# First stage of a two-block network: subtractions and scan sums moved from GpSimd to VectorE

## The chip, the cores and the metric

The kernel runs on one core of one Trainium2 chip. The metric is the device time of one launch in microseconds (us). In this text TensorE is PE, VectorE is DVE, ScalarE is ACT, GpSimd is POOL and SyncE is SP, as the profile has them. Each engine works through its own queue of instructions strictly in order and waits at an instruction until what that one needs is there.

## The reference, cut to what matters

Two blocks of different design follow each other on 512 tokens of width 1024. The change lies in the first block, in its state-space branch and in the multiplication of weights.

```python
def s5_ssm(u, a_re, a_im, log_dt, b_re, b_im, c_re, c_im, d, glu_w, glu_b):
    ...
    bu_r = jnp.einsum('blgp,gnp->blgn', uf, bbar_r)
    bu_i = jnp.einsum('blgp,gnp->blgn', uf, bbar_i)
    ...
    _, _, s_r, s_i = lax.associative_scan(_complex_linear_combine, (a_r, a_i, bu_r, bu_i), axis=1)
    y = (jnp.einsum('blgn,gpn->blgp', s_r, c_re.astype(jnp.float32))
         - jnp.einsum('blgn,gpn->blgp', s_i, c_im.astype(jnp.float32))
         + d.astype(jnp.float32).reshape(SSM_GROUPS, SSM_CH) * uf)
    z = jax.nn.gelu(y.reshape(B, L, SSM_WIDTH), approximate=False)
    z = z * jax.nn.sigmoid(z @ glu_w.astype(jnp.float32) + glu_b.astype(jnp.float32))
    return z.astype(u.dtype)

def first_block(...):
    ...
        proj = rms_norm(h, norm1_g[l]) @ w_in[l]
        attn = sliding_window_attention(...)
        ssm = s5_ssm(...)
        mixed = jnp.concatenate([rms_norm(attn, attn_out_g[l]), rms_norm(ssm, ssm_out_g[l])], axis=-1)
        h = h + mixed @ w_out[l]
        h = h + peer_ffn(...)
```

The scan is a complex linear recurrence over 528 positions (16 meta tokens and 512 tokens), with 32 groups of 64 states. After the first block come a feed-forward layer with 16,384 single-neuron experts (peer_ffn) and the second block of two layers, which also reads a memory of 256 rows through keys and values made from weights.

## The kernel before, in words

**Weights in two parts.** Every large matrix product is made of three passes: the weight is loaded as 128x1024 float32 (tile `wraw`), rounded on ACT to a high part (`whi`, line 267), and the rest is a subtraction (`wlo`, line 268). `mm3` multiplies high by high, low by high and high by low (lines 273 to 275). The class `Stream` does this in a fixed order of weights: three `wraw` buffers are loaded ahead, and three `whi` and `wlo` buffers are split ahead. Its field `lo_eng` says which engine subtracts: POOL where it is set, DVE where it is None.

**The first stage** (`phase_a`) runs two Python generators against each other. `ssm()` has 16 turns T, two groups of the scan each; `fill_a()` yields pieces of all other work: `proj_qkv`, then `attention` (four blocks i of 128 tokens), then `memory` (32 weight columns, 24 products with tile `pk` each, 768 in all), then `mix_out` (tile `po`). `finish_a` comes after both: the gate of the state-space branch (tile `pg`), its half of the output product, and the norm. What the queues finally hold is set by a scheduler that lays all instructions on a simulated time line and orders each engine's queue by it, so an edit in one place can move instructions far from it.

**One turn of the scan.** `table(T)` makes the cosine and sine of 528 positions from two short tables: four products on POOL (lines 653 to 656), one subtraction and one sum on DVE (657, 658). `bu(T)` multiplies on PE (671) and takes each PSUM result times the tables on DVE (673 to 677), combines (679, 680), scans twice (`tensor_tensor_scan`, 683 and 684), multiplies the states by the tables again (687 to 690), and then adds and subtracts these products on POOL:

```python
            g.tensor_tensor(n[0], n[0], n[1], op=OP.add)
            g.tensor_tensor(n[2], n[2], n[3], op=OP.subtract)
```

`y(T)` multiplies both sums on PE (703, 704), and every fourth turn DVE adds the skip term into `uT` (707), which `finish_a` puts through Gelu. One attention block reads scores of PE on DVE (817), takes the softmax through ACT (827, 836) and DVE (831, 832), transposes and multiplies on PE (849, 851, 855), and splits the result (`ahl`, 862 and 863), which `mix_out` needs.

**Before the turns** `norm_in` and `proj_u` normalise the input and project it; their first weights are subtracted on POOL. `ssm_params` makes the angles in eight 128x736 operations on POOL (tile `eq`, 557 to 564), from which ACT takes sine and cosine (569 to 571). `memory_in` puts two small norm chains (319 to 324) into the same queue. In `memory` every call of the stream sets `lo_eng` to POOL, so its 32 weight columns are subtracted there.

**After the stage** `phase_p1` computes expert scores; its DVE routes tokens and handles 128 gathered rows (`ring`, line 1116) and then 128 sums (`sacc`, 1126) for the first token tile. `phase_p2` multiplies the second expert matrix (tile `acc`), and its first step on DVE is line 1289.

Of the kernel before, what the change touches and what calls it, by code (L numbers as in the profile page):

```python
# [17 lines left out]
OP = mybir.AluOpType  # L18
# [185 lines left out]
class Stream:  # L204
# [38 lines left out]
    def next(self, held=0):  # L243

        n = self.n_used
        self._split(n + 1 + self.ahead - held)
        self.n_used += 1
        return self.got.pop(n)


class Kernel:
# [249 lines left out]
    def proj_u(self):  # L501
        nc = self.nc
        self.uT = self.pa.tile([128, 4, L], F32, name="uT")
        norm = self.norm_in()
        for cs in ((0, 1), (2,), (3,)):
            self.W.lo_eng = nc.gpsimd if cs[0] < 1 else None
            ws = [self.W.next(held=j) for j in range(len(cs))]
            for o in HALVES:
                next(norm, None)
                for c, w in zip(cs, ws):  # L510
                    ps = self.proj(w, *o)
                    nc.scalar.copy(self.uT[:, c, o[0]:o[1]], ps)
# [126 lines left out]
    def ssm(self):  # L639
        nc, pa = self.nc, self.pa  # L640
        v, g, pe = nc.vector, nc.gpsimd, nc.tensor
        NA, NB = self.NA, self.NB
        new = lambda n, b=2, w=L: pa.tile([128, w], F32, name=n, tag="s_" + n, bufs=b)
        live = {}

        def table(T):

            sh = [128, NA, NB]
            cA, sA = (x[:, T, :NA, None].to_broadcast(sh) for x in (self.cosS, self.nsinS))
            cB, sB = (x[:, T, None, NA:].to_broadcast(sh) for x in (self.cosS, self.nsinS))  # L650
            c, s, t1, t2 = new("c"), new("s"), new("t1", 1), new("t2", 1)
            r = lambda x: x.rearrange("p (a b) -> p a b", a=NA)
            g.tensor_tensor(r(c), cA, cB, op=OP.mult)
            g.tensor_tensor(r(t1), sA, sB, op=OP.mult)
            g.tensor_tensor(r(s), sA, cB, op=OP.mult)
            g.tensor_tensor(r(t2), cA, sB, op=OP.mult)
            v.tensor_tensor(c, c, t1, op=OP.subtract)
            v.tensor_tensor(s, s, t2, op=OP.add)
            live[T] = [c, s]

        def bu(T):
            a, b = divmod(T, 4)
            c, s = live[T]
            bT = pa.tile([128, 2, 128], F32, name="bT", bufs=2)
            nc.sync.dma_start(out=bT, in_=self.a["bT"][T])
            m = [new(f"m{i}", 1) for i in range(4)]
            for h in range(2):
                hs = slice(h * 264, h * 264 + 264)
                for i in range(2):
                    p = self.ps.tile([128, 264], F32, tag="bu", name="bu", bufs=2)  # L670
                    pe.matmul(p, bT[:, i], self.uT[:, a, hs], start=True, stop=True)
                    if i == 0:
                        v.tensor_tensor(m[0][:, hs], p, c[:, hs], op=OP.mult)
                        v.tensor_tensor(m[3][:, hs], p, s[:, hs], op=OP.mult)
                    else:
                        v.tensor_tensor(m[1][:, hs], p, s[:, hs], op=OP.mult)
                        v.tensor_tensor(m[2][:, hs], p, c[:, hs], op=OP.mult)

            v.tensor_tensor(m[0], m[0], m[1], op=OP.subtract)
            v.tensor_tensor(m[2], m[2], m[3], op=OP.add)  # L680
            mg = self.mag[:, T:T + 1].to_broadcast([128, L])
            sr, si = m[1], m[3]
            v.tensor_tensor_scan(sr, mg, m[0], 0.0, op0=OP.mult, op1=OP.add)
            v.tensor_tensor_scan(si, mg, m[2], 0.0, op0=OP.mult, op1=OP.add)
            n = [new(f"n{i}", 2 - i % 2, S) for i in range(4)]
            o = slice(NM, L)
            v.tensor_tensor(n[0], sr[:, o], c[:, o], op=OP.mult)
            v.tensor_tensor(n[1], si[:, o], s[:, o], op=OP.mult)
            v.tensor_tensor(n[2], sr[:, o], s[:, o], op=OP.mult)
            v.tensor_tensor(n[3], si[:, o], c[:, o], op=OP.mult)  # L690

            g.tensor_tensor(n[0], n[0], n[1], op=OP.add)
            g.tensor_tensor(n[2], n[2], n[3], op=OP.subtract)
            live[T] = [n[0], n[2]]

        def y(T):
            a, b = divmod(T, 4)
            zr, zi = live.pop(T)
            if b == 0:
                for i, x in enumerate((self.cre, self.cim)):  # L700
                    self.fill_pad(self.cpad[i], x, a)
                self.py = self.ps.tile([128, S], F32, tag="y", name="py", bufs=1)
            pe.matmul(self.py, self.cpad[0][:, b], zr, start=(b == 0), stop=False)
            pe.matmul(self.py, self.cpad[1][:, b], zi, start=False, stop=(b == 3))
            if b == 3:
                u = self.uT[:, a, NM:]
                v.scalar_tensor_tensor(u, u, self.ssd[:, a:a + 1], self.py, op0=OP.mult, op1=OP.add)

        table(0)
        for T in range(17):  # L710
            if T + 1 < 16:
                table(T + 1)
            if T < 16:
                bu(T)
            if T >= 1:
                y(T - 1)
            yield 12.0
# [174 lines left out]
    def memory(self):  # L892

        nc, pa = self.nc, self.pa
        pe = nc.tensor
        self.mkd = [self.dram.tile([128, 8, 256], F32, name=f"mk{l}") for l in range(2)]
        self.mvd = [self.dram.tile([128, 2, D], F32, name=f"mv{l}") for l in range(2)]
        mh, ml = self.mhl
        for l in range(2):
            for n in range(16):  # L900
                self.W.lo_eng = self.nc.gpsimd
                w = self.W.next()
                self.W.lo_eng = None
                ps = self.bank("pk")
                for k in range(KC):
                    ks = slice(k * 128, (k + 1) * 128)
                    self.mm3(ps[:, :256], (w[0][:, ks], w[1][:, ks]), (mh[:, k], ml[:, k]), k == 0, k == KC - 1)
                ev = pa.tile([128, 256], F32, name="kev", tag="kev", bufs=2)
                nc.scalar.copy(ev, ps[:, :256])
                if n < 8:  # L910
                    nc.scalar.dma_start(out=self.mkd[l][:, n], in_=ev)
                else:
                    pt = self.bank("pk", (128, 2, 128), "pt")
                    for t in range(2):
                        pe.transpose(pt[:, t], ev[:, t * 128:t * 128 + 128], self.ident)
                    ev = pa.tile([128, 2, 128], F32, name="vev", tag="kev", bufs=2)
                    nc.scalar.copy(ev, pt)
                    nc.scalar.dma_start(out=self.mvd[l][:, :, (n - 8) * 128:(n - 7) * 128], in_=ev)
                yield 2.6
# [1039 lines left out]
```

## Time and profile before

| | before |
|---|---|
| median of 3 runs | 3660.84 us (3656.49 to 3661.97) |
| profiled execution, own time | 3660.37 us |
| its span | 3658.6 us |
| DVE busy over the span | 2597.9 us (71%) |
| POOL busy over the span | 1349.2 us (37%) |
| PE busy over the span | 3309.3 us (90%) |
| `wlo` on DVE | 352 of 1273 ns mean |
| `wlo` on POOL | 171 of 2547 ns mean |

The span is from the first to the last instruction; 1.8 us of the execution lie around it. Shares over the whole span mix stages with different limits, so the stage of the change has to be read by itself, by windows. The mean of a group of instructions holds what they stand still once begun; what an engine idles ahead of an instruction is counted apart, with the work that ended it.

### The profile page before, as it was taken

The page shows a single profiled execution, that of the slowest core. Times are in us where ns is not written, and L with a number is a line of the kernel's source. Part 1 is how long each engine was busy: PE and PEld are TensorE (multiplying, and loading weights), DVE is VectorE, ACT ScalarE, POOL GpSimd, SP SyncE. Part 2 cuts the span into 40 slices and gives each one's busy share as a digit, 9 for nine tenths or more (in the row PEclk, how much of TensorE's full clock was granted, in tenths as well). Part 3 has the DMA queues.
Part 4 walks back from the last instruction along what each step waited for, and adds up shares of the span by engine and source line. Part 5 has one row for each costly group of instructions (what it writes and reads, how often), then busy time and mean ns, then how long its engine had stood idle before and what let it go on. Part 6 is the DMA issues. An engine that isn't in the chain of part 4 may idle for free.

```text
span 3658.6 us, 47432 instructions
## 1 busy us (share of the span) xinstructions
PE 3309.3 (90%) x17407; PEld 2782.9 (76%) x17407; DVE 2597.9 (71%) x5062; ACT 1325.2 (36%) x2267; POOL 1349.2 (37%) x1284
## 2 busy tenths in 40 slices
PE   6877999889889785888999999999999999999998
PEld 5666789878777764666888887788888877888886
DVE  8999447999999998898555777455543686455533
ACT  4234433233233231223333366334431475334431
POOL 6577112662652643674122145431101245331101
PEclk9888999899989886999999999999999999999999
DMA  3222233975875866998665311322222311313322
GB/s 123 85 72 84 88 115 130 320 261 203 300 253 210 305 244 231 347 360 320 225 219 173 130 41 47 115 81 88 95 96 98 126 36 41 133 65 104 98 92 75
DMA packets 173867, 569.87 MB, mean 156 GB/s; under 512 B 18864, under 2 KB 52657, under 8 KB 167617
## 3 DMA queue, kind: packets, MB, share of 16 engines
q1 hardware_dynamic: 114576, 352.37, 28.6%
q0 software_dynamic: 40752, 157.30, 12.0%
q10 hardware_dynamic: 18304, 57.15, 4.1%
q8 instruction: 137, 2.24, 0.3%
q14 instruction: 98, 0.80, 0.1%
HBM read 503.33 MB, written 63.44 MB: 155 GB/s over the span
## 4 chain that ended last, share of the span: by engine, by line
PE 56%; DVE 28%; issue 7%; POOL 5%; DMA 2%; ACT 2%; SPq 0%; DVEq 0%; POOLq 0%; ACTq 0%
PE pl L273 7%; PE pl L274 7%; PE pl L275 7%; DVE ring L1116 4%; PE acc L274 4%; PE acc L275 4%; PE acc L273 3%; DVE wlo L268 2%; DVE O L1252 2%; PE mm L273 2%; PE mm L274 2%; PE mm L275 2%; DVE O L1253 2%; DVE O L1251 2%; DVE sacc L1126 1%
## 5 line engine op out<-in xcount | busy, mean ns | idle before, releaser
L267 ACT CAST whi<-wraw 128x1024 fp32r<-128x1024 f32 x523 | 544.7, 1047 | 950.4 <-PE pl L274 347.6
L268 DVE TENSOR_TENSOR wlo<-wraw,whi 128x1024 fp32r<-128x1024 f32 x352 | 448.0, 1273 | 522.5 <-ACT whi L267 508.3
L268 POOL TENSOR_TENSOR wlo<-wraw,whi 128x1024 fp32r<-128x1024 f32 x171 | 435.2, 2547 | 774.6 <-ACT whi L267 770.2
L275 PE MATMUL pl<-hhi,wlo 128*128 128x384 f32 (+1 forms) x1128 | 408.8, 365 | 64.3 <-POOL wlo L268 37.8
L273 PE MATMUL pl<-hhi,whi 128*128 128x384 f32 (+1 forms) x1128 | 407.9, 362 | 7.6 <-ACT whi L267 7.6
L274 PE MATMUL pl<-hlo,whi 128*128 128x384 f32 (+1 forms) x1128 | 404.6, 359 | 0.0
L274 PE MATMUL pl<-xTlo,whi 128*128 128x512 f32 x944 | 370.3, 392 | 0.0
L273 PE MATMUL pl<-xThi,whi 128*128 128x512 f32 x944 | 369.9, 392 | 0.0
L275 PE MATMUL pl<-xThi,wlo 128*128 128x512 f32 x944 | 367.4, 390 | 0.0
L274 PE MATMUL acc<-wlo,ahl 128*128 128x512 f32 x744 | 299.6, 403 | 21.6 <-DVE wlo L268 16.7
L273 PE MATMUL acc<-whi,ahl 128*128 128x512 f32 x744 | 254.7, 399 | 49.6 <-ACT ahl L267 28.8
L275 PE MATMUL acc<-whi,ahl 128*128 128x512 f32 x744 | 295.6, 400 | 0.0
L275 PEld LDWEIGHTS pl<-hhi,wlo 128*128 128x128 f32 x1128 | 225.1, 200 | 77.0 <-POOL wlo L268 41.9
L1107 POOL DMA_INDIRECT ring<-in_peer_v,sidx x128 | 180.6, 1411 | 199.1 <-DVE sacc L1126 136.1
L273 PEld LDWEIGHTS pl<-hhi,whi 128*128 128x128 f32 x1128 | 225.7, 200 | 18.9 <-ACT whi L267 10.2
L1107 POOL DMA_INDIRECT ring<-in_peer_r,sidx x128 | 169.3, 1323 | 165.4 <-DVE dots L1116 89.9
L274 PEld LDWEIGHTS pl<-hlo,whi 128*128 128x128 f32 x1128 | 225.1, 200 | 4.1
L1940 POOL TENSOR_TENSOR cv<-cv 128x512 f32<-128x512 f32 x44 | 57.1, 1297 | 430.7 <-ACT cv L1939 430.7
L273 PEld LDWEIGHTS acc<-whi,ahl 128*128 128x128 f32 x744 | 139.9, 189 | 88.5 <-ACT ahl L267 29.1
L273 PEld LDWEIGHTS pl<-xThi,whi 128*128 128x128 f32 x944 | 177.2, 188 | 39.0 <-issue 0.5
L275 PEld LDWEIGHTS pl<-xThi,wlo 128*128 128x128 f32 x944 | 177.2, 188 | 38.7 <-issue 0.5
L274 PEld LDWEIGHTS pl<-xTlo,whi 128*128 128x128 f32 x944 | 177.3, 188 | 36.7 <-issue 1.0
(698 smaller groups left out, 7937.5 us busy)
## 6 DMA issues: line engine op xcount, KB each, us to landing
wraw<-in_peer_u SPq DMA_DIRECT2D x128, 512.0 KB
wraw<-in_peer_v SPq DMA_DIRECT2D x128, 512.0 KB
wraw<-in_up SPq DMA_DIRECT2D x88, 512.0 KB
adram<-A ACTq DMA_DIRECT2D x64, 384.0 KB
A<-adram SPq DMA_DIRECT2D x16, 1536.0 KB
gdram<-G ACTq DMA_DIRECT2D x12, 2048.0 KB
G<-gdram SPq DMA_DIRECT2D x16, 1536.0 KB
wraw<-in_down SPq DMA_DIRECT2D x44, 512.0 KB
```

Of the source, the lines that this page charges most:

```text
L267: self.nc.scalar.copy(hi, src)
L268: (eng or self.nc.vector).tensor_tensor(lo, src, hi.bitcast(F32), op=OP.subtract)
L273: mm(out, l[0], r[0], start=start, stop=False)
L274: mm(out, l[0], r[1], start=False, stop=False)
L275: mm(out, l[1], r[0], start=False, stop=stop)
L1107: nc.gpsimd.indirect_dma_start(out=self.ring[n % R], out_offset=None, in_=src[n // 128], in_offset=bass.IndirectOffsetOnAxis(ap=self.sidx[ ...
L1116: v.tensor_tensor_reduce(r, r, self.hs, 1.0, 0.0, op0=OP.mult, op1=OP.add, accum_out=dots[:, n:n + 1])
L1126: v.scalar_tensor_tensor(self.sacc, r, w, self.sacc, op0=OP.mult, op1=OP.add)
L1251: v.tensor_scalar(O[:, 0, j], self.iotab, i1, None, op0=OP.is_equal)
L1252: v.tensor_scalar(Ow[:, j], self.iota, i2, ga, op0=OP.is_equal, op1=OP.mult)
L1253: v.tensor_scalar(O[:, 3, j], self.iotab, i2, gb, op0=OP.is_equal, op1=OP.mult)
L1940: nc.gpsimd.tensor_tensor(ts[0], ts[0], ts[1], op=OP.mult)
```

## The change

Three places of the first stage: the stream no longer hands the subtraction to POOL in `proj_u` (three weights) and in `memory` (32 weights), and the two sums of each of the 16 scan turns are issued on DVE. POOL keeps the four table products of each turn, the `eq` operations and the small norms. `phase_p1` still sets `lo_eng` for every second expert weight.

```diff
         for cs in ((0, 1), (2,), (3,)):
-            self.W.lo_eng = nc.gpsimd if cs[0] < 1 else None
             ws = [self.W.next(held=j) for j in range(len(cs))]
...
-            g.tensor_tensor(n[0], n[0], n[1], op=OP.add)
-            g.tensor_tensor(n[2], n[2], n[3], op=OP.subtract)
+            v.tensor_tensor(n[0], n[0], n[1], op=OP.add)
+            v.tensor_tensor(n[2], n[2], n[3], op=OP.subtract)
             live[T] = [n[0], n[2]]
...
             for n in range(16):
-                self.W.lo_eng = self.nc.gpsimd
                 w = self.W.next()
-                self.W.lo_eng = None
                 ps = self.bank("pk")
```

The scheduler orders all queues anew. In the changed program's listing, lines from 507 on are one lower, and from 901 on two and three lower.

**First place: POOL ahead of the turns.** Tile `eq` is the angles' chain, `rqm` to `rqt` the small norms of the memory, which wait for DVE. Before:

```order
L268 TENSOR_TENSOR wlo<-wraw,whi 128x1024
L557 TENSOR_TENSOR eq<-lv,fh 128x736
L268 TENSOR_TENSOR wlo<-wraw,whi 128x1024
L559 TENSOR_SCALAR eq<-eq 128x736
L268 TENSOR_TENSOR wlo<-wraw,whi 128x1024
L560 TENSOR_SCALAR eq<-eq 128x736
L561 TENSOR_TENSOR eq<-eq 128x736
L319 TENSOR_SCALAR rqm<-bag 128x1 x2
L563 TENSOR_TENSOR eq<-lv,fl 128x736
```

The same place in the changed program:

```order
L556 TENSOR_TENSOR eq<-lv,fh 128x736
L558 TENSOR_SCALAR eq<-eq 128x736
L559 TENSOR_SCALAR eq<-eq 128x736
L560 TENSOR_TENSOR eq<-eq 128x736
L562 TENSOR_TENSOR eq<-lv,fl 128x736
L563 TENSOR_TENSOR eq<-eq 128x736
L319 TENSOR_SCALAR rqm<-bag 128x1
L558 TENSOR_SCALAR eq<-eq 128x736
```

The three `wlo` are gone from this queue, and the norms' first step stands behind two more `eq` operations than before.

**Second place: DVE in a turn of the scan**, from the second scan to the next turn's first PSUM product. Names `m` are the scan's, `n` the products of its states. Before:

```order
L684 SCALAR_TENSOR_TENSOR m_2352<-mag,m_2351 128x528
L687 TENSOR_TENSOR n_2373<-m_2350,c 128x512
L689 TENSOR_TENSOR n_2375<-m_2350,s 128x512
L673 TENSOR_TENSOR m_2553<-bu,c 128x264
L688 TENSOR_TENSOR n_2374<-m_2352,s 128x512
L690 TENSOR_TENSOR n_2376<-m_2352,c 128x512
L676 TENSOR_TENSOR m_2554<-bu,s 128x264
L677 TENSOR_TENSOR m_2555<-bu,c 128x264
L831 TENSOR_TENSOR sm<-sm,es 128x8
```

The same turn in the changed program:

```order
L268 TENSOR_TENSOR wlo<-wraw,whi 128x1024
L683 SCALAR_TENSOR_TENSOR m_2352<-mag,m_2351 128x528
L686 TENSOR_TENSOR n_2373<-m_2350,c 128x512
L688 TENSOR_TENSOR n_2375<-m_2350,s 128x512
L672 TENSOR_TENSOR m_2553<-bu,c 128x264
L687 TENSOR_TENSOR n_2374<-m_2352,s 128x512
L689 TENSOR_TENSOR n_2376<-m_2352,c 128x512
L675 TENSOR_TENSOR m_2554<-bu,s 128x264
L676 TENSOR_TENSOR m_2555<-bu,c 128x264
L691 TENSOR_TENSOR n_2373<-n_2373,n_2374 128x512
L692 TENSOR_TENSOR n_2375<-n_2375,n_2376 128x512
L673 TENSOR_TENSOR m_2556<-bu,s 128x264
```

The two sums follow the four products at once, and a `wlo` stands between the scans. From the first to the last turn's first scan DVE's queue held 5 `wlo` and now holds 38.

**Third place: DVE at the last scan's end.** `oG` and `ahl` belong to attention, `uT` is the branch's result, `pS` the scores. Before:

```order
L683 SCALAR_TENSOR_TENSOR m_3443<-mag,m_3442 128x528
L684 SCALAR_TENSOR_TENSOR m_3445<-mag,m_3444 128x528
L687 TENSOR_TENSOR n_3466<-m_3443,c 128x512
L689 TENSOR_TENSOR n_3468<-m_3443,s 128x512
L688 TENSOR_TENSOR n_3467<-m_3445,s 128x512
L690 TENSOR_TENSOR n_3469<-m_3445,c 128x512
L861 TENSOR_TENSOR oG<-oT,pack_486 128x512
L707 SCALAR_TENSOR_TENSOR uT<-uT,pack_486,py 128x512
L332 TENSOR_SCALAR rwm<-pr 128x1
L863 TENSOR_TENSOR ahl<-oG,ahl 128x4x128
L333 TENSOR_SCALAR rwy<-rwm 128x1
L817 ISA s,mx<-pS,pack_486,rq 128x256
```

The same place in the changed program:

```order
L682 SCALAR_TENSOR_TENSOR m_3443<-mag,m_3442 128x528
L683 SCALAR_TENSOR_TENSOR m_3445<-mag,m_3444 128x528
L831 RECIPROCAL rr<-sm 128x8
L686 TENSOR_TENSOR n_3466<-m_3443,c 128x512
L688 TENSOR_TENSOR n_3468<-m_3443,s 128x512
L687 TENSOR_TENSOR n_3467<-m_3445,s 128x512
L689 TENSOR_TENSOR n_3469<-m_3445,c 128x512
L691 TENSOR_TENSOR n_3466<-n_3466,n_3467 128x512
L692 TENSOR_TENSOR n_3468<-n_3468,n_3469 128x512
L706 SCALAR_TENSOR_TENSOR uT<-uT,pack_486,py 128x512
L268 TENSOR_TENSOR zhl<-uT,zhl 128x512
L860 TENSOR_TENSOR oG<-oT,pack_486 128x512
```

Before, the scores of the last attention block (`pS`, with `oG` and `ahl` of the block ahead of it) come behind the last scan. Now that block's scores lie ahead of the last scans, and its last softmax step (`rr`) stands between them and the products. On PE, 120 of the 768 `pk` products came after the last `bu` product before; none does now, and the first `po` follows the last block at once. In the queue of DVE 35 of the `sacc` sums stood ahead of the first line-1289 product of `phase_p2`; now 23 do. From the start of the second block on, all queues are as before.

## Rows read from the trace of the kernel before

**Rows 1.** Windows of the first stage: busy us of each engine, granted clock, DMA.
```profile
0.00:76.86 76.86, 41.46 (x262) 37.61 (x263) 63.59 (x166) 32.67 (x57) 51.29 (x58) 0.89 0.40 137
76.86:369.10 292.24, 232.41 (x1333) 194.01 (x1332) 277.79 (x408) 99.76 (x212) 195.50 (x117) 0.88 0.24 78
369.10:402.69 33.59, 28.88 (x215) 25.79 (x214) 12.93 (x41) 22.45 (x51) 10.18 (x6) 0.90 0.32 99
```
**Rows 2.** Groups by line, 76.86 to 369.10 us: busy us, mean ns, idle before.
```profile
L268 POOL TENSOR_TENSOR wlo<-wraw,whi 128x1024 fp32r<-128x1024 f32 x28 | 73.0, 2609 | 15.3 <-ACT whi L267 15.2
L692 POOL TENSOR_TENSOR n<-n,n 128x512 f32<-128x512 f32 x16 | 27.4, 1715 | 70.1 <-DVE n L688 63.0 <-DVE rwt L336 4.8 <-PE pt L915 2.2
L693 POOL TENSOR_TENSOR n<-n,n 128x512 f32<-128x512 f32 x16 | 24.4, 1524 | 0.0
```
**Rows 3.** The same view, DVE's lines.
```profile
L683 DVE TENSOR_TENSOR_SCAN m<-mag,m 128x528 f32<-128x528 f32 x16 | 26.3, 1641 | 0.0
L684 DVE TENSOR_TENSOR_SCAN m<-mag,m 128x528 f32<-128x528 f32 x16 | 26.0, 1622 | 0.0
L680 DVE TENSOR_TENSOR m<-m,m 128x528 f32<-128x528 f32 x15 | 21.6, 1442 | 0.0
L657 DVE TENSOR_TENSOR c<-c,t 128x528 f32<-128x528 f32 x14 | 20.2, 1441 | 1.1 <-POOL c L653 1.1
L679 DVE TENSOR_TENSOR m<-m,m 128x528 f32<-128x528 f32 x15 | 19.9, 1329 | 0.0
L658 DVE TENSOR_TENSOR s<-s,t 128x528 f32<-128x528 f32 x14 | 19.4, 1383 | 3.8 <-POOL s L655 3.7
...
L268 DVE TENSOR_TENSOR wlo<-wraw,whi 128x1024 fp32r<-128x1024 f32 x5 | 8.5, 1692 | 0.4 <-ACT whi L267 0.4
```
**Rows 4.** Timeline of DVE where nothing holds it up: start us, us, instruction.
```profile
62.73 1.21 DVE L268 TENSOR_TENSOR wlo<-wraw,whi 128x1024 fp32r<-128x1024 f32 x1
63.87 0.69 DVE L657 TENSOR_TENSOR c<-c,t 128x528 f32<-128x528 f32 x1
...
76.86 1.25 DVE L683 TENSOR_TENSOR_SCAN m<-mag,m 128x528 f32<-128x528 f32 x1
...
79.17 0.67 DVE L687 TENSOR_TENSOR n<-m,c 128x512 f32<-128x512 f32 x1
79.76 0.69 DVE L689 TENSOR_TENSOR n<-m,s 128x512 f32<-128x512 f32 x1
```
**Rows 5.** Timeline of POOL and DVE where both run at once.
```profile
205.82 2.38 POOL L268 TENSOR_TENSOR wlo<-wraw,whi 128x1024 fp32r<-128x1024 f32 x1
205.90 2.86 DVE L658 TENSOR_TENSOR s<-s,t 128x528 f32<-128x528 f32 x1 [0.60 <-POOL s L655]
...
209.86 1.07 POOL L653 TENSOR_TENSOR c<-cosS 128x528 f32<-128x528 f32 x1
```
**Rows 6.** Timeline ahead of the turns.
```profile
10.26 2.39 DVE L336 TENSOR_TENSOR rwt<-rwt,rwm 128x1 f32<-128x1 f32 x2
...
22.64 2.30 DVE L336 TENSOR_TENSOR rwt<-rwt,rwm 128x2 f32<-128x2 f32 x1
...
33.79 0.46 POOL L319 TENSOR_SCALAR rqm<-bag 128x1 f32<-128x1 f32 x2 [4.96 <-DVE bag L932]
```
**Rows 7.** Timeline of the last attention block, up to the first `po`.
```profile
389.34 0.20 DVE L832 RECIPROCAL rr<-sm 128x8 f32<-128x8 f32 x1
...
394.60 0.65 PE L849 MATMUL pT<-ident,s 128*128 128x128 f32 x4
...
402.56 0.48 PE L273 MATMUL po<-whi,ahl 128*128 128x512 f32 x1
```
**Rows 8.** Windows of `phase_p1` and the first part of `phase_p2`, columns as in rows 1.
```profile
600.00:1438.00 838.00, 689.44 (x4124) 620.91 (x4122) 812.98 (x2191) 248.25 (x362) 381.50 (x233) 0.88 0.72 253
1438.00:1700.00 262.00, 221.22 (x888) 170.54 (x888) 234.31 (x238) 73.09 (x100) 165.63 (x102) 0.97 0.93 347
```
**Rows 9.** Groups by line, DVE, 600 to 1438 us.
```profile
L1126 DVE SCALAR_TENSOR_TENSOR sacc<-ring,dots,sacc 128x1024 f32<-128x1024 f32 x35 | 51.1, 1461 | 3.6 <-DMA ring<-in_peer_v,sidx 3.3
```

## The prediction

> **What bounds the kernel now.** The change lies in the first stage, so I cut the span by windows there first, at the first scan, the last scan's sums and the first `po` product [rows 1]. In the middle stretch of 292.2 us, the 16 turns, DVE is busy 277.8 us, 95%; PE is busy 232.4 and POOL 195.5. DVE sets the pace. In the third stretch, 33.6 us, DVE is busy only 12.9 and PE 28.9: there the last attention block and leftover memory columns hold up `mix_out`.
>
> Next I asked what DVE's busy time consists of, from the groups by line [rows 3] against the same shapes where nothing holds DVE up [rows 4]. A 128x528 operation takes 0.69 alone and 1.33 to 1.44 on average in the turns; a scan takes 1.25 alone and 1.64 or 1.62. So 16 x 0.39 + 16 x 0.37 + 15 x 0.75 + 14 x 0.75 + 15 x 0.64 + 14 x 0.69 = 53 us of these six lines, and 5 x 0.48 = 2 us of `wlo`, are standing still. The pair in the timeline shows how [rows 5]: POOL's `wlo` starts at 205.82 and ends at 208.20, and DVE's table sum, begun 0.08 later, lasts to 208.76, 2.86 instead of 0.69. One ran, then the other. Of the turns' 292 us at least 56, almost a fifth, is DVE waiting behind POOL inside its own instructions.
>
> **The change part by part.** The sum is made against the profiled execution's own 3660.37 us, 0.5 us under the median. About 0.2%, 7 us, is what a measurement of this kernel can tell from no change.
>
> *A, ahead of the turns.* Three POOL `wlo` go. Each stops DVE's small norm steps for some 2.3 us, the first at 10.26 and the last at 22.64 [rows 6]; three `wlo` on DVE cost 1.14 each, the step between the two starts in rows 4. That is 3.4 - 6.9 = -3.5. POOL's norm step also waited 4.96 us for DVE with the rest of the angles' chain behind it [rows 6]; it now stands later in that queue. How much of this reaches the first scan the trace does not show: between none and all. With half, A = -6; bounds 0 and -10.
>
> *B, the turns, added on DVE.* 33 more `wlo` stand between the first and the last turn's first scan (38 against 5): 28 from POOL in this stretch [rows 2], the rest from the tail. 33 x 1.14 = 37.6. The 32 sums: one product's start to the next is 0.59 [rows 4], so 32 x 0.59 = 18.9. The last block's scores move ahead of the last scan: about half of DVE's 12.9 in the third stretch [rows 1], 7. Together +63.5.
>
> *B, removed.* The 56 us of standing still come from all POOL work, 195.5 us: 73.0 `wlo`, 51.8 sums [rows 1, 2], about 70 table products. By length, 37% or 21 us are due to `wlo`. Upward, were each of 28 like the pair, 28 x 2.17 = 61, more than all there is. I take 40, a little above the middle: a long POOL instruction catches a DVE instruction nearly always, and a 1.07 us product [rows 5] less often. For the sums, between 0 and 26%, 15 us, I take 8. DVE also idles 3.8 + 1.1 us for table products [rows 3], which came late because sums and `wlo` stood ahead of them on POOL; 4.9 go. So B = 63.5 - 40 - 8 - 4.9 = +11. With 56 and 15 removed instead it is -12.
>
> *C, behind the last scan.* Before, the first `po` comes 33.6 us after the last sums, as the last block's softmax, 120 `pk` products and the block's values stand in between. In the new order `rr` of that block lies before the last products. From `rr` at 389.34 to the first transpose at 394.60 [rows 7] PE did `pk`; without these I allow 2 us for ACT's first scaling. From the transpose to the first `po` is 8.0 [rows 7]. So `po` starts 10 us after `rr`. The products and sums behind `rr` take 6 x 0.59 = 3.5, hence `po` comes 6.5 us after the last sum, and with Gelu, which now shares ACT's queue there, some 8.6. C = 8.6 - 33.6 = -25. If columns come late, what is left of them delays it: bounds -10 and -28.
>
> *D, later.* `phase_p1` is DVE-bound, 813 of 838 us [rows 8]. Twelve fewer `sacc` stand ahead of `phase_p2`, each 1.46 [rows 9]: -17.5. They run in the next stretch instead, where DVE is busy 234 of 262 and PE idles 41 [rows 8], so much is given back. I take a third, -6; bounds -17 and +5, since the reshuffled order can also lose.
>
> The stream's loads are in the same order and end 3 ahead of use as before; POOL's indirect gathers stand behind the stage; ACT's roundings are the same in number. I cost these at nothing: they lie behind DVE's turns, and would cost only if DVE ran dry.
>
> Sum: -6 + 11 - 25 - 6 = -26, so **3634 us**.
>
> **The rivals.**
>
> *Relief in full.* All 56 us go with `wlo` and sums: B = -12, the sum -49, **3611**. For it: DVE waits behind POOL to the end in the pair [rows 5]. Against: table products remain, and stop DVE too.
>
> *The waits move to DVE.* POOL itself waited 15.2 us for `whi` [rows 2], off the path. Now DVE stands there with the scan queued behind, and every late column stops the recurrence; PE works in order too, and its `bu` products stand between more `pk`. B then is +26, and part of the columns' work is still late, C = -10: -6 + 26 - 10 - 6 = +4, **3664**, no change. For it: DVE already waits 5.0 us for the `bu` products of PE in the same turns, and PE has only 60 idle us of 292 [rows 1]. Against: DVE waited merely 0.4 for `whi` in its own `wlo` [rows 3].
>
> *The tables lock out DVE.* With sums and `wlo` on it, more of DVE's queue has two SBUF inputs, and the four products of some 14 turns, 56 x 1.07 = 60 us, could each stop it for their whole length, against some 8 to 10 now. B = 11 + 50 = +61, the sum +24, **3684**, slower. For it: 205.90 [rows 5]. Against: before, products often ran beside PSUM work. It decides if the mean of lines 657, 658, 679 and 680 stays above 1.3 with only tables on POOL. [...]
>
> *No relief.* The standing still is not POOL's doing, or comes back wholly: DVE takes 63.5 more, the sum +26.5, **3687**, slower. Against it speaks the pair [rows 5]. [...]
>
> **How the numbers follow.** Forecast, 3634 (between 3653 and 3615): 0.62, as two gains, fewer and shorter locks and the shorter tail, have separate grounds. Relief in full: 0.12. Waits move to DVE: 0.14. Tables lock out: 0.08. No relief: 0.04. Faster by over 0.2%: 0.62 + 0.12 = 0.74; within: 0.14; slower: 0.08 + 0.04 = 0.12. The range reaches from 3606, full relief with C at its better end and a little more, to 3660, where the third case begins; the slower cases, 0.12, and some of the third are left out.
>
> **What would show it.** In the changed profile, lines 656, 657, 678 and 679 (their new numbers) should fall from about 1.4 towards 0.9 to 1.0, DVE's `wlo` to about 1.2 to 1.3 in the turns, and POOL's share to about a third. The turns should last 295 to 310 us, DVE still over 90% busy. From the last sum to the first `po` should be about 9 us with no `pk` in it. If DVE shows more than 10 us of idle time ahead of `wlo` behind ACT's `whi`, the second rival holds. If the first stage ends 30 us sooner and the whole does not, D is wrong: then `phase_p1` or `phase_p2` has lost by the new order.

## The result, and the profile of the changed kernel

The changed kernel takes 3622.8 us in the median of 4 runs (3619.14 to 3626.72); the kernel before takes 3659.4 beside it. The ratio is 0.990, 95% interval [0.9883, 0.9918]. It is 37 us faster; 3634 had been predicted, with a range from 3606 to 3660. The profiled execution's own time is 3619.14 us.

The page of the changed kernel: the span, its engines, and the groups of `wlo`. Line numbers are one lower than before from line 507 on, and three lower from 904 on.

```profile
span 3617.3 us, 47426 instructions
...
PE 3294.8 (91%) x17407; PEld 2763.7 (76%) x17407; DVE 2568.3 (71%) x5129; ACT 1322.6 (37%) x2266; POOL 1207.9 (33%) x1217
...
L268 DVE TENSOR_TENSOR wlo<-wraw,whi 128x1024 fp32r<-128x1024 f32 x387 | 492.4, 1273 | 511.9 <-ACT whi L267 497.7
L268 POOL TENSOR_TENSOR wlo<-wraw,whi 128x1024 fp32r<-128x1024 f32 x136 | 347.7, 2559 | 762.0 <-ACT whi L267 746.1
```

DVE has taken over 35 `wlo` and 32 sums and is nevertheless busy 30 us less than before (2597.9). The windows below are cut at the first scan, the end of the last sum, the first `po` product, the first `acc` product, and the first `identb` step, which opens the second block. Columns are start and end, length, then busy us (and instructions) of PE, PE's weight load, DVE, ACT and POOL, then granted clock, DMA share, GB/s.

```profile
0.00:73.95 73.95, 40.07 (x254) 36.19 (x255) 63.94 (x167) 31.12 (x55) 46.94 (x55) 0.95 0.40 140
73.95:365.30 291.35, 244.13 (x1491) 201.45 (x1490) 275.87 (x512) 116.78 (x256) 83.37 (x58) 0.93 0.29 90
365.30:376.22 10.92, 10.22 (x65) 6.52 (x63) 2.13 (x3) 5.25 (x9) 0.00 (x0) 0.77 0.00 0
376.22:1379.20 1002.98, 868.26 (x5123) 777.27 (x5122) 877.98 (x2429) 317.06 (x474) 381.25 (x273) 0.91 0.64 225
1379.20:2003.50 624.30, 567.52 (x2385) 449.58 (x2386) 449.69 (x477) 190.82 (x262) 264.73 (x187) 0.97 0.76 270
```

Against [rows 1], the turns stay at 291 us with DVE busy 276 instead of 278, and POOL falls from 195.5 to 83.4 busy us there. The tail falls from 33 to 11 us. The groups of DVE in the turns of the changed kernel (busy us, mean ns, idle before):

```profile
L268 DVE TENSOR_TENSOR wlo<-wraw,whi 128x1024 fp32r<-128x1024 f32 x38 | 51.3, 1350 | 2.0 <-ACT whi L267 1.9
L682 DVE TENSOR_TENSOR_SCAN m<-mag,m 128x528 f32<-128x528 f32 x16 | 19.9, 1245 | 0.0
...
L656 DVE TENSOR_TENSOR c<-c,t 128x528 f32<-128x528 f32 x14 | 15.1, 1079 | 0.0
L692 DVE TENSOR_TENSOR n<-n,n 128x512 f32<-128x512 f32 x16 | 14.4, 900 | 0.0
...
L672 DVE TENSOR_TENSOR m<-bu,c 128x264 f32<-128x264 f32 x30 | 12.6, 421 | 6.9 <-PE bu L670 6.9
...
L675 DVE TENSOR_TENSOR m<-bu,s 128x264 f32<-128x264 f32 x30 | 12.5, 417 | 4.9 <-PE bu L670 4.8
...
L657 DVE TENSOR_TENSOR s<-s,t 128x528 f32<-128x528 f32 x14 | 10.6, 758 | 1.0 <-POOL s L654 1.0
...
L678 DVE TENSOR_TENSOR m<-m,m 128x528 f32<-128x528 f32 x15 | 10.4, 695 | 0.0
```

The combining step (line 678) is down from the 1.33 us of [rows 3] to 0.695, its undisturbed length, and the scan from 1.64 to 1.245. What still stands are the `wlo` (1.350 against 1.22 undisturbed), the table subtraction 656 (1.079 against 0.70) and the moved sums (0.900 at 692 against 0.68): they meet POOL's table products.

For all kernels below I worked out from the traces how long DVE was **held**: for each DVE instruction beside which a POOL instruction ran, its duration less what the same line with the same shape takes in its shortest tenth, put down to the POOL instruction that overlaps it most. The columns of lengths are the five stretches of the windows above; then come the held us in the turns by `wlo`, sums and table products, and those in the fourth stretch by `wlo`. r1 and r2 are second traces of the two kernels. Where a kernel ran once, its one time is given.

| kernel | time | ahead | turns | tail | `po` to `acc` | `acc` to `identb` | held in turns | held, 4th |
|---|---|---|---|---|---|---|---|---|
| before | 3660.8 | 76.9 | 292.5 | 33.2 | 1035.5 | 608.1 | 52, 11, 23 | 125 |
| r1 | 3664.6, one run | 76.5 | 292.8 | 34.2 | 1036.0 | 607.9 | 51, 9, 24 | 125 |
| changed | 3622.8 | 74.0 | 291.3 | 10.9 | 1003.1 | 624.3 | 0, 0, 23 | 107 |
| r2 | 3623.7, one run | 75.0 | 289.9 | 10.8 | 1001.7 | 625.8 | 0, 0, 23 | 107 |
| e1 | 3626.0 | 76.8 | 282.1 | 23.2 | 1006.4 | 625.4 | 0, 15, 24 | 110 |
| e2 | 3646.0 | 76.6 | 293.8 | 27.6 | 1012.1 | 622.0 | 55, 0, 22 | 113 |
| e3 | 3663.1 | 74.3 | 297.5 | 32.3 | 1032.9 | 605.9 | 54, 10, 21 | 116 |
| e4 | 3599.6 | 74.5 | 291.2 | 10.0 | 1009.0 | 599.6 | 0, 0, 23 | 0 |
| g1 | 3627.7 | 77.3 | 290.3 | 32.5 | 1011.4 | 597.7 | 53, 11, 22 | 0 |
| f1 | 3597.6 | 75.0 | 290.1 | 10.8 | 1006.7 | 590.2 | 0, 0, 23 | 0 |
| f2 | 3604.8 | 72.7 | 302.5 | 10.8 | 1006.9 | 591.8 | 0, 0, 0 | 0 |
| f3 | 3626.0, one run | 76.8 | 271.8 | 16.2 | 1019.7 | 623.0 | 18, 13, 20 | 117 |
| f4 | 3612.6, one run | 76.9 | 254.8 | 30.1 | 1031.2 | 604.1 | 2, 16, 19 | 119 |
| g2 | 3667.7 | 76.8 | 291.2 | 33.2 | 1032.8 | 614.7 | 52, 10, 23 | 122 |

### The profile page after: what moved, and what is told of

Same layout as the page of the kernel before. It is cut to its first block, busy times and chain, and to the rows that moved or that the text cites. A ratio compares the mean times of both kernels' runs of the same rounds, so it can differ in the third digit from the quotient of the medians.

```text
span 3617.3 us, 47426 instructions
## 1 busy us (share of the span) xinstructions
PE 3294.8 (91%) x17407; PEld 2763.7 (76%) x17407; DVE 2568.3 (71%) x5129; ACT 1322.6 (37%) x2266; POOL 1207.9 (33%) x1217
## 4 chain that ended last, share of the span: by engine, by line
PE 57%; DVE 29%; issue 5%; POOL 5%; DMA 3%; ACT 2%; SPq 0%; DVEq 0%; POOLq 0%; ACTq 0%
PE pl L274 7%; PE pl L273 7%; PE pl L275 7%; PE acc L274 4%; PE acc L275 4%; PE acc L273 3%; DVE ring L1113 3%; DVE wlo L268 3%; DVE O L1249 3%; DVE O L1250 3%; PE mm L273 2%; PE mm L274 2%; PE mm L275 2%; DVE O L1248 2%; PE T L274 2%
## 5 line engine op out<-in xcount | busy, mean ns | idle before, releaser
L268 DVE TENSOR_TENSOR wlo<-wraw,whi 128x1024 fp32r<-128x1024 f32 x387 | 492.4, 1273 | 511.9 <-ACT whi L267 497.7
L268 POOL TENSOR_TENSOR wlo<-wraw,whi 128x1024 fp32r<-128x1024 f32 x136 | 347.7, 2559 | 762.0 <-ACT whi L267 746.1
L1104 POOL DMA_INDIRECT ring<-in_peer_r,sidx x128 | 158.8, 1241 | 158.9 <-DVE dots L1113 61.6
```

What stands on the lines that cost most here:

```text
L268: (eng or self.nc.vector).tensor_tensor(lo, src, hi.bitcast(F32), op=OP.subtract)
L1104: nc.gpsimd.indirect_dma_start(out=self.ring[n % R], out_offset=None, in_=src[n // 128], in_offset=bass.IndirectOffsetOnAxis(ap=self.sidx[ ...
```

## The experiments

**e1, the memory's subtractions alone.**

```diff
             for n in range(16):
-                self.W.lo_eng = self.nc.gpsimd
                 w = self.W.next()
-                self.W.lo_eng = None
```

> The kernel before with one part of the change: the memory's 32 `wlo` on DVE; sums of the products and the three early `wlo` stay on POOL. Theory (a POOL subtraction holds DVE inside its own instructions for 1.7 us, and doing it on DVE costs 1.27 us): the stall by `wlo`, 52 us of the turns, goes and about as much work comes (38 `wlo` at 1.3); the turns last 285 to 295 us, the tail to the first `po` falls from 33.5 to 10 to 14 us, first `po` near 377 to 382, the time 3625 to 3637. Rival (the sums, not the subtractions, hold DVE up): the turns last 310 us or more, and the time is no better than 3650. Rival (only the order of the tail counts): the tail falls, but the means of the DVE lines 657, 679 and 680 stay near 1.4.

Measured: 3626.0 us, ratio 0.990 [0.9885, 0.9913]; the time is as expected. The turns are 10.4 us shorter than before, 282.1 and so below the 285 to 295 set, and the hold by `wlo` is gone. But the tail is 23.2 and not 10 to 14. Its timeline (start us, length, engine, line, instruction):

```profile
357.69 1.26 POOL L693 TENSOR_TENSOR n<-n,n 128x512 f32<-128x512 f32 x1
...
359.65 1.52 PE L813 MATMUL pS<-kz,qT 128*128 128x256 f32 x4
...
363.51 1.28 ACT L827 ACT_TABLE_LOAD   x1
...
369.28 0.20 DVE L832 RECIPROCAL rr<-sm 128x8 f32<-128x8 f32 x1
369.58 3.30 ACT L836 ACTIVATE s<-s,rr 128x256 f32<-128x256 f32 x8
...
373.08 0.80 PE L851 MATMUL oT<-mT,vmb 128*128 128x128 f32 x2 [1.16 <-ACT mT L842]
...
382.19 0.48 PE L273 MATMUL po<-whi,ahl 128*128 128x512 f32 x1
```

With the sums on POOL, the last block's scores stand behind the last sums, and its softmax is over 10 us after them; no `pk` is left in this tail either. So `wlo` alone brings 20.4 us up to the first `po`. The sums bring little more: on DVE they make the turns 9.2 us longer and the tail 12.3 us shorter (e1 against the changed kernel).

**e2, the sums alone.**

```diff
-            g.tensor_tensor(n[0], n[0], n[1], op=OP.add)
-            g.tensor_tensor(n[2], n[2], n[3], op=OP.subtract)
+            v.tensor_tensor(n[0], n[0], n[1], op=OP.add)
+            v.tensor_tensor(n[2], n[2], n[3], op=OP.subtract)
```

> The kernel before with one part of the change: the two sums of each turn on DVE; all `wlo` stay where they were. Theory: the sums' stall (10.6 us) and the table products that came late (4.9 us) go, 18.9 us of work come; the turns last 292 to 300 us, the tail stays at 30 us or more since the memory's columns remain late, and the time is 3650 to 3665, no difference beyond 0.3%. Rival (the sums hold DVE up): the turns fall by 20 us or more, and the time to 3635 or less.

Measured: 3646.0, ratio 0.9956 [0.9942, 0.997]. The turns (293.8) and the hold by `wlo` (55) came as the theory has it, but the time is 4 us below what I had allowed, a miss: the tail is 6 us shorter (27.6, where 30 or more had been set), and the two later stretches together 9.5 us. The parts do not add up: e1, e2 and e3 against their own runs of before make -34.7, -14.8 and +2.4, together -47 where the whole change makes -37. In the two later stretches alone e1, e2 and e3 gain 11.8, 9.5 and 4.8, together 26, where the whole change gains 16.2; by these 10 us the parts exceed the whole.

**e3, the three early subtractions alone.**

```diff
-            self.W.lo_eng = nc.gpsimd if cs[0] < 1 else None
```

> The kernel before with one part of the change: the three early `wlo` on DVE. Theory: the first scan comes 2 to 5 us sooner, as in the whole change (3.2), and nothing else changes; where five more `sacc` stand ahead of the first product of the last phase (40 instead of 35) that product comes later, by up to 7 us, and the later phase makes about half of it good. Time 3655 to 3664. Rival (the early part carries the gain through the order of what follows): 3645 or less.

Measured: 3663.1, ratio 1.0009 [1.0, 1.0018]. The time is as expected, and the first scan comes 2.5 us sooner. But nothing else was to change, and the turns lose 5.0 while the two later stretches gain 4.8; why is not shown.

**e4, the same exchange in `phase_p1`.** Its edit, on the changed kernel:

```diff
-            self.W.lo_eng = nc.gpsimd if n % 2 else None
+            self.W.lo_eng = None
```

> The changed kernel, and phase_p1's 64 `wlo` that POOL still does on DVE as well: the same exchange in a phase without a tail of this kind. Theory: in phase_p1 of the changed kernel 61 POOL `wlo` hold DVE up for 1.76 us each, 107 us together; on DVE they cost 61 x 1.27 = 77 us; DVE's time up to the first product of the last phase falls by some 20 to 35 us, counted without the 34 more `sacc` that stand ahead of it (57 instead of 23, 1.46 us each, which the last phase then saves), and the whole is 3590 to 3612. Rival (order and tail made the gain, and DVE only takes on work): up to 77 us slower than the changed kernel, 3650 to 3700.

Measured: 3599.6, ratio 0.983 [0.9815, 0.9844]: faster than either kernel, as the theory has it and against the rival by 50 us and more. Three of DVE's groups from the first `po` to the first `acc`, in r1, in the changed kernel, and in e4:

```profile
L1116 DVE CUSTOM_DVE_ANT_0 ring<-ring,hs 128x1024 f32<-128x1024 f32 x128 | 189.8, 1498 | 7.0 <-DMA ring<-in_peer_r,sidx 7.0
L1252 DVE TENSOR_SCALAR O<-pack,T,g 128x128 f32<-128x128 f32 x384 | 147.7, 390 | 0.0
...
L1126 DVE SCALAR_TENSOR_TENSOR sacc<-ring,dots,sacc 128x1024 f32<-128x1024 f32 x35 | 51.2, 1462 | 3.6 <-DMA ring<-in_peer_v,sidx 3.4
```

```profile
L1113 DVE CUSTOM_DVE_ANT_0 ring<-ring,hs 128x1024 f32<-128x1024 f32 x128 | 186.1, 1464 | 6.0 <-DMA ring<-in_peer_r,sidx 5.9
L1249 DVE TENSOR_SCALAR O<-pack,T,g 128x128 f32<-128x128 f32 x384 | 142.3, 376 | 0.0
...
L1123 DVE SCALAR_TENSOR_TENSOR sacc<-ring,dots,sacc 128x1024 f32<-128x1024 f32 x23 | 31.5, 1371 | 4.0 <-DMA ring<-in_peer_v,sidx 3.6
```

```profile
L1113 DVE CUSTOM_DVE_ANT_0 ring<-ring,hs 128x1024 f32<-128x1024 f32 x128 | 153.5, 1215 | 7.5 <-DMA ring<-in_peer_r,sidx 6.4 <-issue 1.0
L1249 DVE TENSOR_SCALAR O<-pack,T,g 128x128 f32<-128x128 f32 x384 | 129.6, 346 | 0.0
...
L1123 DVE SCALAR_TENSOR_TENSOR sacc<-ring,dots,sacc 128x1024 f32<-128x1024 f32 x57 | 72.8, 1276 | 7.3 <-DMA ring<-in_peer_v,sidx 7.1
```

Once no POOL `wlo` is beside them, the `ring` instruction falls from 1.46 to 1.22 us, `sacc` from 1.37 to 1.28 and the one-hot step `O` from 0.376 to 0.346.

**g1, `phase_p1` without POOL, but the first stage as before.** The edit is e4's, on the kernel before.

> The kernel before, the first stage untouched, but phase_p1's 64 `wlo` of POOL on DVE, as in e4. It asks why the later phases gained 15 us with the change (D). From the first `po` product to the first `identb`, before takes 1643.6 us, the change 1627.4, e4 1608.6. Theory (`sacc` that move from one phase to the next cost nothing either way; the gain is that POOL's 64 `wlo` of phase_p1 happened to hold DVE for 107 instead of 125 us): without these 64 the gain is gone too; this stretch takes 1603 to 1615 as in e4, and the time is e4's 3600 plus the first stage's 26, 3618 to 3634. Rival (fewer `sacc` ahead of the last phase, or an earlier start, gained the 15 us): e4's lead over this kernel stays at the change's 37 to 42, 3636 to 3650.

Measured: 3627.7, ratio 0.9917 [0.9903, 0.993], inside the theory's range and outside the rival's. From `po` to `identb` g1 takes 1609.1 us and e4 1608.6: with POOL's 64 `wlo` gone from `phase_p1`, the change of the first stage gains nothing more behind it. g1 and e4 have nearly the same number of `sacc` ahead of `acc` too, 58 and 57, so that g1 alone does not tell the hold from that number.

**f1, `phase_p2` too.** On e4:

```diff
-            self.W.lo_eng = nc.gpsimd if n % 3 == 2 or n == 125 else None
+            self.W.lo_eng = None
```

> e4, and the `wlo` that POOL still does in phase_p2 (41) on DVE as well. Theory: these hold DVE for 72 us there and would cost it 41 x 1.25 = 51; DVE gets 21 us, but PE is busy most of that phase too, so half or less arrives: 3583 to 3597 against e4's 3600. Rival (PE sets that phase's pace): 3597 to 3605, no difference.

Measured: 3597.6 (3591.45 to 3600.54), ratio 0.9827 [0.9813, 0.984]. Against e4 that is no difference that these runs can tell: the ratios' intervals cover each other almost wholly. The windows from `acc` to `identb`, e4's and then f1's:

```profile
1384.60:1984.20 599.60, 561.03 (x2398) 446.19 (x2399) 408.10 (x443) 189.99 (x261) 215.46 (x153) 0.99 0.71 252
```

```profile
1382.50:1972.80 590.30, 559.18 (x2375) 446.89 (x2376) 383.70 (x485) 190.68 (x262) 103.62 (x111) 0.98 0.72 256
```

DVE has 24 us less to do, and PE is busy 559 of 590 us. The stretch is 9.3 us shorter in f1's trace, but f1's traced execution, 3591.58, is one of its quickest, and f2 below, with POOL's `wlo` still in that stretch, has 591.8 there. The median lies where the ranges of theory and rival meet: PE's pace fits, but f1 does not decide between no gain and a small one.

**f2, the table products too.** On e4, the four `g.tensor_tensor` of `table` become `v.tensor_tensor`:

```diff
-            g.tensor_tensor(r(c), cA, cB, op=OP.mult)
+            v.tensor_tensor(r(c), cA, cB, op=OP.mult)
...
```

> e4, and the four table products of each turn on DVE too, so that POOL computes nothing in the turns. It asks where the exchange stops paying. Theory (POOL's price to DVE is what it holds it for): the products hold DVE for 23 us and make it idle for 1 or 2; on DVE they cost 64 x 0.6 = 38; the turns last 5 to 22 us longer than e4's 291, the time is 3605 to 3622, and DVE's instructions of the turns run at their undisturbed lengths (0.69 for 128x528, 1.25 for a scan). Rival (what still lies over the undisturbed lengths is not POOL's): the lengths stay and the turns take the whole 38 us more.

Measured: 3604.8, ratio 0.9853 [0.9838, 0.9868], 5 us above e4, with intervals that overlap by a little, and just under the theory's 3605; the turns last 302.5, 11.3 more, as the theory has it. DVE's groups in the turns:

```profile
L268 DVE TENSOR_TENSOR wlo<-wraw,whi 128x1024 fp32r<-128x1024 f32 x38 | 46.3, 1220 | 0.9 <-ACT whi L267 0.9
...
L692 DVE TENSOR_TENSOR n<-n,n 128x512 f32<-128x512 f32 x16 | 10.9, 680 | 0.0
...
L656 DVE TENSOR_TENSOR c<-c,t 128x528 f32<-128x528 f32 x14 | 9.7, 696 | 0.0
```

Every line now has its undisturbed length: all that had stood still in the turns was POOL's doing. And the exchange has turned: the 54 products of the turns held DVE for 23 us and cost it 33, 0.62 each, counted from the end of the instruction before to their own end.

**f3 and f4, what of a POOL instruction holds DVE.** Both on the kernel before; for the memory's 32 columns the subtraction becomes one of these, which leaves out the low parts of the memory's weights:

```diff
+            eng.tensor_scalar(lo, hi.bitcast(F32), 0.0, None, op0=OP.mult)
```

```diff
+            eng.memset(lo.bitcast(F32), 0.0)
```

> The kernel before; POOL's 32 `wlo` of the memory's columns are no subtraction of two tiles but a multiplication of one (whi) by zero, written to the same place; the low parts of the memory's weights are left out so. Theory (what holds DVE is any POOL instruction that reads SBUF): DVE is held for a time in proportion to the instruction's length, 0.5 to 0.9 of it, so with the subtraction's 2.6 us still some 50 us, with one of 1.2 us some 20. Rival (it is the two inputs): DVE's stall by these falls below 10 us however long they take, and lines 657 and 679 fall from 1.4 to about 1.1.

> The kernel before; POOL's 32 `wlo` of the memory's columns are a memset to the same place, which reads nothing; the low parts of the memory's weights are left out so. With the subtraction they hold DVE for 52 us of the turns, with one input read (f3) for 18. Theory (what is shared is reading): below 5 us; the turns last 255 to 275 us. Rival (writing holds DVE too): 10 us or more.

Measured, f3: on POOL the instruction with one input takes 3.10 us on average, longer than the subtraction's 2.61 [rows 2], and holds DVE for 18 instead of 52 us. That lies between theory and rival; neither named it. Of the turns' DVE instructions with two SBUF inputs (lines 657, 658, 679, 680, 683, 684, 687 to 690 of before), r1 has 33 that ran beside a `wlo` of POOL for over 0.1 us, 30 of them held, by 1.60 us on average. In f3 it is 69, of which 25 were held, by 0.77 on average and never more than 0.89. f3 changes POOL's operation together with the number of its inputs; which of the two makes the difference is not shown. A piece of f3's timeline, where two such POOL instructions run one after the other:

```profile
183.40 6.45 POOL L270 TENSOR_SCALAR wlo<-whi 128x1024 fp32r<-128x1024 f32 x2
...
185.32 0.69 DVE L662 TENSOR_TENSOR s<-s,t 128x528 f32<-128x528 f32 x1
185.93 0.68 DVE L691 TENSOR_TENSOR n<-m,c 128x512 f32<-128x512 f32 x1
...
187.14 1.52 DVE L692 TENSOR_TENSOR n<-m,s 128x512 f32<-128x512 f32 x1
```

Three instructions with two inputs ran through at full speed (the one left out too), the fourth was held by 0.84. In f4 the memset (0.95 us) holds DVE for 2.4 us in all, as expected, and the turns last 254.8, at the lower edge of the 255 to 275 set; the scan at 163.57 runs through beside it:

```profile
163.57 1.24 DVE L687 TENSOR_TENSOR_SCAN m<-mag,m 128x528 f32<-128x528 f32 x1
163.80 0.95 POOL L270 MEMSET wlo<- 128x1024 f32 x1 [0.45 <-PE pk L279]
```

**g2, r1 and r2, how firm the later gain is.** g2 is the kernel before with

```diff
-            self.W.lo_eng = nc.gpsimd if n % 2 else None
+            self.W.lo_eng = None if n % 2 else nc.gpsimd
```

> The kernel before with phase_p1's alternation turned round: POOL does the low part of the even columns instead of the odd ones, 64 as before. The first stage's time stays (first `po` within 3 us of 402). Theory (by how much POOL's 64 subtractions hold DVE up depends on what DVE happens to do then, and the later time follows it one for one): the held time in phase_p1 differs from before's 125 us, and the stretch from the first `po` product to the first `identb` differs from 1643.6 by the same amount, to 6 us. Rival: the held time changes by 10 us or more and the stretch does not follow, or the other way round.

> The kernel before once more, for a second trace: whether the held time in phase_p1 (125 us), that of the turns by `wlo`, sums and tables (52, 11, 23) and the tail (33.2) are the kernel's or a run's. Theory: each repeats within 5 us. Rival: they scatter by 10 us or more, and then the 15 us of the later phases are not explained by them.

> The changed kernel once more, for a second trace: held time in phase_p1 107 us, in the turns by tables 23, the tail 10.9, the stretch from the first `po` product to the first `identb` 1627. Theory: each repeats within 5 us. Rival: they scatter by 10 us or more.

Measured: r1 and r2 repeat each value within 3 us, the held time in `phase_p1` to 1 us (125.3 and 107.3). g2 takes 3667.7, ratio 1.002 [1.001, 1.0029]. Its held time is 3 us less than before's, and its stretch from `po` to `identb` 3.9 us more (1647.5): 7 us apart, just outside what I had allowed. The held time is the kernel's own, but it does not set the later time one for one.

## Why the prediction was right, step by step

The sum was made of A -6, B +11, C -25, D -6. The profile shows -2.9, -1.2, -22.3, -16.2, in all -42.6 up to `identb`; 1.3 us are lost again later, and the profiled execution ended 41.2 sooner. The direction and its reason in the first stage hold. B and D were mis-sized, by 12 and 10 us, both to the better side, and D's sign, as far as the traces tell, came from something other than its reason: that was luck. The signs named ahead were met only in part: the turns last 291 us and not 295 to 310, DVE's `wlo` take 1.35 and not 1.2 to 1.3.

**A** (-6): -2.9 in the trace, -1.6 in r2 against r1, -2.5 in e3. The half that was to come from the holds, -3.5, did not: the 6.5 us of hold by `wlo` are gone, but `wlo` on DVE take 4.2 and POOL's other work now holds DVE for 2 more, so that DVE's busy time stays (64). The half from waits did, -3.3: DVE's idle time falls from 13.3 to 10.0.

**B** (+11): -1.2. The added work was right: the 38 `wlo` make 51.3 us against 8.5, 42.8 more with what POOL's tables still hold them up, where 37.6 undisturbed had been set; the sums take 19.2 undisturbed, where 18.9 had been set; by undisturbed lengths all of DVE's work in the turns rose by 67, where 63.5 had been set. What failed is the removed side, "56 us" of standing still and "40" of it due to `wlo`. The 56 counted six lines and five `wlo`; over all of DVE's lines it was 86, since small steps were held as well (a maximum over 128x8 took 1.79 us beside a `wlo` in r1, and takes 0.16 in e1). And the split by POOL's own busy time gave `wlo` 37%, where it had caused 52 of the 86 us, 60%: 29 `wlo` held DVE for 1.80 each, 32 sums for 0.33, the 54 table products for 0.42. Taken by holds, `wlo` and sums give back 63, not 48. Against it the 4.9 us of DVE's waits for tables did not go over into time: they fell to 1.0, but those behind PE's `bu` rose from 5.5 to 11.7, and DVE's idle time in the turns is 14.5 us before and 15.5 after (16.2 and 14.1 in r1 and r2).

The exchange rate explains DVE's busy time in the turns. A `wlo` held DVE for 1.80 and costs it 1.14 [rows 4]: moving it gains. A sum held it for 0.33 and costs 0.60: moving it loses 19.2 - 10.6 = 8.6 us, and in e2 DVE is busy 9.7 more (287.5). In e1 the sums held DVE for 15, so that 4 us are worked out from e1 to the changed kernel, and DVE is busy 5.3 more (270.6 to 275.9). A table product holds for 0.42 and costs 0.62: in f2 DVE is busy 9.4 us more than in e4 (276.6 to 286.0) where 33 - 23 = 10 is worked out. The length of the turns follows less closely, since DVE's idle time moves as well: in e2 it falls by 8 us and the turns grow by only 1.3, from e1 to the changed kernel it rises by 4 and they grow by 9.2.

**C** (-25): -22.3. The last block's `rr` lies 4 us ahead of the last sum's end (3.5 set), and no `pk` is in the tail. The step that was too short is from `rr` to the first `po`, 14.9 us instead of 10. The timeline of the changed kernel, then a window of it (columns as above), then ACT's scalings and a window of the kernel before:

```profile
361.35 0.17 DVE L831 RECIPROCAL rr<-sm 128x8 f32<-128x8 f32 x1
361.62 3.31 ACT L835 ACTIVATE s<-s,rr 128x256 f32<-128x256 f32 x8 [3.20 <-DVE rr L831]
362.40 0.47 PE L839 MATMUL pmT<-ident,mP 128*128 128x128 f32 x1 [5.40 <-POOL mP L833]
362.67 1.06 PE L848 MATMUL pT<-ident,s 128*128 128x128 f32 x4
...
364.75 2.08 PE L702 MATMUL py<-n,cpad 128*128 128x512 f32 x2 [1.02 <-DVE n L691]
...
367.90 1.92 PE L703 MATMUL py<-n,cpad 128*128 128x512 f32 x2
...
368.75 1.28 ACT L956 ACT_TABLE_LOAD   x1
...
376.22 0.48 PE L273 MATMUL po<-whi,ahl 128*128 128x512 f32 x1
```

```profile
361.35:369.80 8.45, 6.38 (x17) 3.44 (x17) 3.95 (x8) 5.57 (x12) 0.65 (x1) 0.50 0.01 3
```

```profile
390.21 3.30 ACT L836 ACTIVATE s<-s,rr 128x256 f32<-128x256 f32 x8
...
394.60:402.56 7.96, 7.26 (x71) 5.88 (x70) 1.92 (x2) 4.63 (x10) 0.00 (x0) 0.99 0.45 146
```

The first transpose comes 1.3 us after `rr`, but the last turn's four `py` products, 4.0 us, stand between the block's transposes and its values in PE's queue, and Gelu's table load on ACT falls into the same stretch. Before, the 8.0 us from the transpose to `po` held neither. They explain only part: in e1 neither stands there, and `rr` to `po` takes 12.9 us all the same. The 8.0 us came from a stretch where two things were otherwise. ACT's eight scalings were over before the first transpose; in e1 and in the changed kernel they take 3.3 us beside it, and the block's first `oT` product (373.08 in e1) waits for a copy that stands behind them in ACT's queue. And PE's granted clock was 0.99, behind 5.3 us at 0.50 in which PE was busy with `pk` for 5.2. In the changed kernel, where PE had idled 5.4 us ahead of 362.40, it is 0.50 from `rr` on for 8.5 us, and four transposes take 1.06 us instead of 0.65. In e1, where PE had idled 8.6 us ahead of the block's first transposes, four take 1.06 us as well, and the tail's granted clock is 0.67. What sets the clock no run shows by itself. How the 2.9 us of e1 divide between the two is not shown. No run shows the 2.1 us that the sum sets for Gelu by themselves.

**D** (-6): -16.2. The step read: twelve fewer `sacc` ahead of `acc` save 17.5 us, and two thirds of that are given back. The reordering was foreseen rightly, 35 to 23, but all of it is given back: counted without overlaps, `sacc` take DVE 18.5 us less ahead of `acc` and 18.2 more behind it (18.6 and 15.5 from r1 to r2). Kernels with other counts say the same: e3 and f4 have 40 `sacc` there and are 5 and 8 us quicker than before from `po` to `identb`, f3 has 29 and is only 1 quicker. What fell together with the time is the hold in `phase_p1`, 125 to 107 us by the same 64 POOL `wlo`, which meet other DVE instructions once the queues have shifted; and where those 64 are gone, the old first stage (g1) and the new one (e4) are followed by stretches that agree to 0.5 us. Over the ten traces with those 64 on POOL, the stretch from `po` to `identb` goes with the held time (correlation 0.91) more than with the number of `sacc` ahead of `acc` (0.68). So I take most of D for a by-product of where the holds happen to fall. g1 and the traces speak for it, but no edit changes the hold alone, so it is argued and not shown. Nor do the two go together exactly: g2 and f3 are each some 7 us off a one-to-one rule, and f2 is 10 us quicker than e4 there with equal holds. What moves these last 10 us, mostly in `phase_p2`, stays open.

**The rivals.** The waits that move to DVE: 1.9 us of idle time behind ACT's `whi` in the turns, far from the 15.2 and the 10 that were to decide. The tables that lock DVE out: their hold is 22.9 before and 22.6 after, only on other lines, and 656, 657, 678 and 679 stand at 1.08, 0.76, 0.70 and 0.70, not above 1.3. No relief fell with 678, back to 0.695. Relief in full was to bring B to -12, but that sum takes away 56 and 15 where all of the 56 was to be 56: by its own words B is 63.5 - 56 - 4.9 = +2.6 and the time 3626, not 3611. What came was 63 us given back out of 86, and B at -1. The time, 3623, lies nearer to that 3626 than to the forecast's 3634, though 10 us of it came from D, which no rival had.

## What to carry to other kernels

The offload from DVE to POOL had a price here that stood nowhere as a wait: how long POOL's instruction held DVE inside DVE's own instructions, 86 us in the turns of the kernel before. Read it by comparing each line's mean with the same line undisturbed, over all lines, the small steps too, and set it against what the work costs on DVE: moving back paid for the long subtraction of two SBUF tiles (1.80 against 1.14 us) and not for short products (0.42 against 0.62). That rate tells the engine's busy time; the stage's time also depends on what the engine then waits for (e2). Where the engine to be freed is not the bound, freeing it further may buy nothing: with DVE in `phase_p2` (f1), busy 384 of 590 us, the runs show no gain that they can tell.

## What the runs showed that was not expected

**One input, and PSUM.** That a POOL instruction with one SBUF input, though it ran for 3.1 us, let 44 of 69 two-input DVE instructions through unhindered was not expected. DVE's work on PSUM turned out wholly free of it: all 23 multiplications from `bu` and score steps from `pS` that ran beside a POOL `wlo` in r1's turns took their undisturbed time. A piece of r1's timeline:

```profile
341.40 0.42 DVE L673 TENSOR_TENSOR m<-bu,c 128x264 f32<-128x264 f32 x1
341.42 2.36 POOL L268 TENSOR_TENSOR wlo<-wraw,whi 128x1024 fp32r<-128x1024 f32 x1
341.74 0.41 DVE L674 TENSOR_TENSOR m<-bu,s 128x264 f32<-128x264 f32 x1
342.08 0.47 DVE L817 CUSTOM_DVE_ANT_0 s<-pS,pack,rq 128x256 f32<-128x256 f32 x1
```

On POOL's side, the same 128x1024 output held DVE in the turns for 52 us where it was made from two SBUF inputs (before), for 18 from one (f3, none of the 69 by more than 0.89) and for 2.4 from none (f4). What in the hardware makes the difference no run shows.

**Where it is cheap.** The POOL subtraction cost DVE nothing at 341.42 in r1 (2.36 us long), beside PSUM work, and 2.2 us at 205.90 (2.38 us long) [rows 5], beside a table sum. It was not tried whether an order that puts POOL's `wlo` beside PSUM work alone would beat e4.
